# One pool of twelve 1024-column tiles for raw, upper and lower weights, in a two-layer hybrid decoder trunk

## The chip, the cores and the metric

The kernel runs on one core of a Trainium2 chip. The core has five engines with an instruction queue each, which this document calls by the profile's names: PE (matmuls; PEld is its weight load, which overlaps), DVE (vector), ACT (scalar), POOL (GpSimd) and SP, whose queue issues nearly all transfers between device memory (HBM) and the on-chip memory (SBUF). Each engine works through its queue in order; semaphores hold an instruction back until what it reads is there or what it overwrites is free. PE's sums go to a third memory (PSUM).

The metric is the device time of one execution in microseconds. The kernel before was run three times: 1729.38, 1731.37 and 1731.99 us, so the median is 1731.37 us.

## The reference

The input is 512 tokens of 1024 float32 numbers; 16 learned tokens are put ahead, so layer 0 and the beginning of layer 1 work on 528 tokens.

```python
for i in range(DEPTH):                       # two layers
    mix = retention_gdn_mixer(h, ...) if i % 2 == 0 else mamba2_mixer(h, ...)
    h = layer_norm(DN_ALPHA * h + mix, ln1_w[i], ln1_b[i])
    h = layer_norm(DN_ALPHA * h + sq_relu_mlp(h, mlp_w1[i], mlp_w2[i]), ln2_w[i], ln2_b[i])
return h[:, N_META:]
```

`retention_gdn_mixer` projects the tokens to 6 x 1024 + 8 columns, runs four retention heads and four gated delta-rule heads in chunks, and projects 2048 columns back to 1024. `mamba2_mixer` projects to 5152 columns, puts 3072 of them through a convolution of four taps and a silu, runs a chunked decay attention in four groups of eight heads (state 128), gates, normalises and projects 2048 columns back. `sq_relu_mlp` is `square(relu(h @ w1)) @ w2` with 4096 hidden columns. All weights are float32 and are read once: some 150 MB.

## The kernel before

**How a product is made.** Everything is kept feature-major: a tile has 128 features as partitions and the tokens as columns. A float32 operand is split into an upper part `hi`, which is the number cast to PE's shorter float32r format, and a lower part `lo`, which is the number minus `hi`, again as float32r. A product of 128 x 128 weights with the tokens is then three matmuls into one PSUM tile (`mm3`): upper weight by upper input (line 173), upper weight by lower input (line 174), lower weight by upper input (line 175). The program has 3296 such triples for its large products, each for 272, 256 or 512 tokens.

**How a weight comes in.** The host lays the weights out so that one load brings 128 x 1024 numbers (512 KB): eight blocks of 128 x 128, which are the eight k-steps of one output tile. `fetch` (line 155) takes a raw tile `wr` (tag of two buffers of 1024 columns) and issues the load on SP. `wload` (line 160) takes the raw tile in two halves of 512 columns; for each it takes an upper tile `wh` and a lower tile `wl` (six buffers of 512 columns each) and calls `split`: a cast on ACT (line 152) and a subtraction on DVE (line 153). There are 253 loads: 245 of 1024 columns, six of 512 columns (lines 1158 and 1164), one of 256 and one of 64. The same `split` is used, outside `wload`, for the input tokens (line 253) and the gated heads (line 920).

**What sets the order.** The kernel is written as one program in which large products (`phase`, `product`) are cut into units; between two units `tick` lets every pending generator emit its next stage (heads, norms, state updates), so that PE has matmuls while other engines prepare a stage. The program is then planned when it is built: a planner plays it through with assumed durations, puts each engine's instructions in the order in which they become ready (earlier ones in the program first), hands out the buffers of a tag in the program's order of first use, and writes the semaphore waits. The durations of the tiles' instructions and the number of buffers thus decide not only waits but the order of every queue.

**Buffers of the weights.** A raw buffer is free again when its two subtractions are done. A `wh` buffer is free when its last upper-weight matmul (line 174) is done, a `wl` buffer when its last lower-weight matmul (line 175) is done. With two raw buffers and six half tiles of each kind, at most two loads are under way or waiting and at most three weight tiles are split. Together these buffers take 8 + 12 + 12 = 32 KB of each SBUF partition. (Lines 70 to 82 give the other tags: 40 tiles `s`, 20 `m`, 40 `n`, 3 `row`; PSUM has three tiles `pmm` and five `pmx`.)

**The stages, in the order of time.** Loads of tokens and first weights, with some matmuls of zeros (to 8 us); layer 0's projections with the heads beside them (to about 400 us); output projection and norm (to 545 us); MLP 0 (to 890 us); norm and layer 1's projections (`conv_tile`, `z_tiles`) with the four groups of the decay attention (`ssd_group`, line 967) beside them (to about 1255 us); output projection, norm, MLP 1 (to 1700 us), and the last norm with the stores.

**The group stage, which the prediction needs.** A conv tile's product goes from PSUM through ACT (`conv_evac`, line 400), ACT (line 405), three multiply-adds on DVE (line 407), ACT (line 408) and DVE (line 410); its result feeds PE transposes, from which DVE makes `xdt` (line 1006). The decays of a chunk come by a load (`row<-rd`), POOL (line 985), ACT (lines 986 and 987) and POOL (line 1001). Then PE makes the chunk's products (lines 1045 and 1049). There are four groups of four chunks, 16 chunks in all. The weight casts and subtractions of the conv tiles stand in the same ACT and DVE queues.

Of the kernel before, what the change touches and what calls it, by code (L numbers as in the profile page):

```python
# [18 lines left out]
P = 128  # L19
# [38 lines left out]
def trunk(ctx: ExitStack, tc: tile.TileContext, a, out):  # L58
# [34 lines left out]
    # ---------------------------------------------------------------- interleaving  # L93
    # The large products are cut into units; between two units every pending task (a generator) emits
    # its next stage, so that the tensor engine works on while other engines prepare a stage's inputs.
# [31 lines left out]
    # ---------------------------------------------------------------- constants  # L127
# [22 lines left out]
    # ---------------------------------------------------------------- weights  # L150
# [3 lines left out]

    def fetch(src, n=1024):
        raw = sb.tile([P, 1024], F32, tag="wr", bufs=2, name=nm("wr"))
        SY.dma_start(raw[:, :n], src)
        return raw

    def wload(src, n=1024, raw=None):  # L160
        if raw is None:
            raw = fetch(src, n)
        res = []
        for i in range(0, n, 512):
            c = min(512, n - i)
            hi = sb.tile([P, 512], F32R, tag="wh", bufs=6, name=nm("wh"))
            lo = sb.tile([P, 512], F32R, tag="wl", bufs=6, name=nm("wl"))
            split(hi[:, :c], lo[:, :c], raw[:, i:i + c])
            res.append((hi, lo))
        return res  # L170
# [6 lines left out]
    def product(o, blks, xs, m=P, k0=0, k1=None, every=8):  # L177
        """o[m, n] += sum over k0 <= k < k1 of blks[k]^T xs[k]"""
        per = 512 // P if m == P else 8
        n = len(xs)  # L180
        for k in range(k0, k1 or n):
            hi, lo = blks[k // per]
            c = (k % per) * m
            mm3(o, (hi[:, c:c + m], lo[:, c:c + m]), xs[k], k == 0, k == n - 1)
            if k % every == every - 1 and k < n - 1:
                tick()

    def phase(tiles, rhs, evac, ns, head=0, tail=0, ready=None):
        """tiles: list of (srcs, key[, m]); rhs[half][k] = (hi, lo) APs, rhs[2] both halves where they fit a
        bank. In the first and the last tiles the halves are apart, so that what precedes and follows can  # L190
        work on one half at a time."""
# [28 lines left out]
    def jobs(lst, rhs, ns, **kw):  # L220
        """phase whose tiles bring their own evac"""
        phase(lst, rhs, lambda ev, hf, o: ev(hf, o), ns, **kw)

    # ---------------------------------------------------------------- h: hi/lo in two halves
# [3 lines left out]
    def parts(pair, spans):  # L228
        """(hi, lo) over the spans of both tiles"""
        return [tuple(x[:, o:o + n] for x in pair) for o, n in spans]  # L230

    # while the first loads are under way, products of zeros let the clock of the tensor engine come up
# [26 lines left out]
    def layernorm(r, ns, hf, go, apply, together=False):  # L259
        """statistics of the tokens of a half as its sums r come, then apply(off, bn, pt, mean, rstd, i)"""  # L260
# [49 lines left out]
    def norm_after(r, ns, wcol, bcol):  # L310
        """tasks for both halves, each from when its sums have been emitted"""
# [35 lines left out]
    def residual(hx, offs, ns, early=()):  # L347
        """evac into r = alpha * h + product"""
# [48 lines left out]
    # ---------------------------------------------------------------- shared pieces  # L397
# [15 lines left out]
    def conv_job(src, wc, bcol, done):  # L413
        """projection through conv and silu, feature-major [128, L]"""
        cin = tl("s", L + 3)
        G.memset(cin[:, 0:3], 0.0)

        def evac(hf, o):
            conv_evac(cin, hf, o)
            if hf == 1:  # L420
                done(conv_silu(cin, wc, bcol))

        return [src], evac
# [21 lines left out]
    def gate_job(src, width, task):  # L445
        """small projection, then a task on its sums"""
# [10 lines left out]
    def gate_task(fm, width):  # L457
        """token-major [128, 5, width] with unused rows zero"""
# [9 lines left out]
    def decay(dt_in, bias, alog, nh):  # L468
        """g = -exp(A_log) softplus(x + bias), sums over chunks and their exponentials"""
# [17 lines left out]
    # ================================================================ layer 0 mixer  # L487
# [15 lines left out]
    # scratch in DRAM for the diagonal blocks of 32: a pitch of 129 rows makes the 68 blocks equidistant  # L503
# [26 lines left out]
    def gdn_keys(hd):  # L530
# [3 lines left out]
        # decays between the tokens of a chunk  # L534
# [16 lines left out]
        # similarities of the keys; the squared norms are on their diagonal  # L551
# [32 lines left out]
    def gdn_base():  # L584
        """diagonal blocks of 32, one to a partition: forward substitution"""
# [349 lines left out]
    # ================================================================ layer 1 mixer  # L935
# [27 lines left out]
    def hb(ap):  # L963
        """[128, heads] over the 64 features of a head"""
        return bc(ap, 64)
# [188 lines left out]
    # the first products begin with the groups that are ready  # L1154
# [20 lines left out]
    def finish(hf):  # L1175
# [16 lines left out]
        def last(blocks):  # L1192
            """both blocks at once, over the engines; what needs the mean alone comes first"""
# [27 lines left out]
# ---------------------------------------------------------------- host side: layout only  # L1221
def _tiles(w, cols):
    """[K, M] -> [M tiles, 128, K] in tiles of 128 columns"""
# [95 lines left out]
```

## Time and profile before

| | us |
|---|---|
| three runs | 1729.38, 1731.37, 1731.99 |
| span of the profiled execution, first to last instruction | 1727.4 |
| PE busy | 1690.1 |
| DVE busy | 1015.5 |
| ACT busy | 680.0 |
| POOL busy | 324.1 |

The span of the profiled execution is 4.0 us below the median of the runs; start and end of an execution, outside the span, are in the runs' times and not in the span. In the page, "busy" is the time in which an engine has an instruction under way. A group is a line of the source on one engine with the tiles that it writes and reads, how often, its busy time, the mean of one, and the idle time of the engine just before it with what ended that idle time. The trace also tells, for any stretch of time, how long each engine was busy in it, and which clock PE was granted (1.00 is full speed).

### The profile page before, as it was taken

How to read it: one execution, taken by the hardware profiler on the slowest of the kernel's cores; microseconds unless marked ns; L12 is line 12 of the kernel's file. 1: busy time of each engine (PE TensorE's matmuls, PEld its weight loads, DVE VectorE, ACT ScalarE, POOL GpSimd, SP SyncE). 2: the span in 40 equal slices, each digit the busy share in tenths (PEclk: the TensorE clock that was granted, in tenths of full speed). 3: DMA queues.
4: the chain of work that ended last, by engine and by line, in shares of the span. 5: the costliest groups of instructions: out<-in, count | busy, mean ns of one | idle time of the engine just before them, and what ended most of it. 6: DMA issues, size and time to landing. Idle time of an engine off the chain costs nothing.

```text
span 1727.4 us, 29456 instructions
## 1 busy us (share of the span) xinstructions
PE 1690.1 (98%) x11644; PEld 1537.0 (89%) x11644; DVE 1015.5 (59%) x2116; ACT 680.0 (39%) x1455; POOL 324.1 (19%) x380
## 2 busy tenths in 40 slices
PE   9999999999999999999999999999999999999997
PEld 8899998899999999999999878888788888888886
DVE  6896667676436443343348767868753744444345
ACT  4432345554225333242425634554432533333331
POOL 1311211010004111010202245242400411101012
PEclk9999999999999999999999999999999999999999
DMA  7224211112222222222221443333222222222221
GB/s 252 69 86 121 77 63 62 38 63 85 98 66 82 92 92 87 98 87 89 96 72 61 131 133 88 99 110 111 80 79 98 73 86 98 98 98 89 94 98 61
DMA packets 80325, 157.99 MB, mean 91 GB/s; under 512 B 12668, under 2 KB 45820, under 8 KB 79932
## 3 DMA queue, kind: packets, MB, share of 16 engines
q1 hardware_dynamic: 80044, 155.86, 28.2%
q8 instruction: 91, 1.49, 0.4%
q14 instruction: 46, 0.38, 0.1%
q10 hardware_dynamic: 144, 0.26, 0.0%
HBM read 149.95 MB, written 6.15 MB: 90 GB/s over the span
## 4 chain that ended last, share of the span: by engine, by line
PE 84%; DVE 6%; DMA 3%; POOL 3%; ACT 2%; issue 2%; SPq 0%; POOLq 0%; DVEq 0%; ACTq 0%
PE pmm L173 24%; PE pmm L175 24%; PE pmm L174 24%; DMA row<-rd 2%; DVE s L407 2%; DVE wl L153 2%; POOL row L985 1%; PE pmx L271 1%; POOL hl L341 1%; DMA wr<-in_w 1%; PE pmx L331 1%; PE pmx L1049 1%; PE pmx L1045 1%; POOL n L147 1%; PE pmx L753 1%
## 5 line engine op out<-in xcount | busy, mean ns | idle before, releaser
L173 PE MATMUL pmm<-hh,wh 128*128 128x272 f32 (+4 forms) x2104 | 652.3, 311 | 2.3 <-ACT wh L152 0.9
L174 PE MATMUL pmm<-hl,wh 128*128 128x272 f32 (+4 forms) x2104 | 638.5, 304 | 2.7 <-POOL hl L341 2.1
L175 PE MATMUL pmm<-hh,wl 128*128 128x272 f32 (+4 forms) x2104 | 640.3, 304 | 0.1
L153 DVE TENSOR_TENSOR wl<-wr,wh 128x512 fp32r<-128x512 f32 (+1 forms) x498 | 376.2, 759 | 319.8 <-ACT wh L152 313.5
L152 ACT CAST wh<-wr 128x512 fp32r<-128x512 f32 (+1 forms) x498 | 306.6, 619 | 628.3 <-PE pmm L174 605.1
L173 PEld LDWEIGHTS pmm<-hh,wh 128*128 128x128 f32 (+2 forms) x2104 | 393.5, 187 | 25.0 <-issue 4.4
L174 PEld LDWEIGHTS pmm<-hl,wh 128*128 128x128 f32 (+2 forms) x2104 | 393.6, 187 | 24.4 <-POOL hl L341 4.6
L175 PEld LDWEIGHTS pmm<-hh,wl 128*128 128x128 f32 (+2 forms) x2104 | 393.5, 187 | 17.0 <-DVE wl L153 0.3
L173 PE MATMUL pmm<-s,wh 128*128 128x256 f32 (+2 forms) x1192 | 377.9, 317 | 0.0
L175 PE MATMUL pmm<-s,wl 128*128 128x256 f32 (+2 forms) x1192 | 377.2, 317 | 0.0
L174 PE MATMUL pmm<-s,wh 128*128 128x256 f32 (+2 forms) x1192 | 376.4, 316 | 0.0
L174 PEld LDWEIGHTS pmm<-s,wh 128*128 128x128 f32 x1192 | 224.3, 188 | 15.5 <-DVE s L1124 0.3
L173 PEld LDWEIGHTS pmm<-s,wh 128*128 128x128 f32 x1192 | 224.4, 188 | 15.1
L175 PEld LDWEIGHTS pmm<-s,wl 128*128 128x128 f32 x1192 | 224.1, 188 | 15.0
L383 POOL TENSOR_TENSOR m<-m 128x256 f32<-128x256 f32 (+1 forms) x128 | 92.1, 729 | 536.0 <-ACT m L381 532.7
L147 POOL TENSOR_TENSOR n<-n,neg 128x1 f32<-128x1 f32 (+2 forms) x58 | 37.9, 657 | 462.7 <-DVE n L146 436.5
L390 DVE TENSOR_TENSOR s<-m,s 128x256 fp32r<-128x256 f32 (+1 forms) x128 | 64.3, 521 | 95.2 <-POOL m L383 93.2
L407 DVE SCALAR_TENSOR_TENSOR s<-s,pp,s 128x528 f32<-128x528 f32 x120 | 96.5, 804 | 25.8 <-ACT s L405 24.1
L363 DVE TENSOR_TENSOR m<-m,pmm 128x256 f32<-128x256 f32 (+1 forms) x108 | 43.7, 423 | 107.4 <-PE pmm L175 107.2
L381 ACT ACTIVATE m<-pmm 128x256 f32<-128x256 f32 (+1 forms) x128 | 48.7, 380 | 60.4 <-PE pmm L175 60.4
L985 POOL TENSOR_TENSOR row<-row,m 128x1024 f32<-128x1024 f32 x16 | 32.8, 2052 | 122.3 <-DMA row<-rd 78.3
L389 ACT ACTIVATE s<-m 128x256 fp32r<-128x256 f32 (+1 forms) x128 | 54.0, 422 | 3.9
(275 smaller groups left out, 1501.1 us busy)
## 6 DMA issues: line engine op xcount, KB each, us to landing
wr<-in_mw SPq DMA_DIRECT2D x128, 512.0 KB, 3.3
wr<-in_w SPq DMA_DIRECT2D x88, 512.0 KB, 3.3
wr<-in_wo SPq DMA_DIRECT2D x29, 512.0 KB, 3.5
row<-rd SPq DMA_DIRECT2D x16, 512.0 KB, 6.0
s<-rd SPq DMA_DIRECT2D x32, 128.0 KB, 6.1
out<-row SPq DMA_DIRECT2D x7, 256.0 KB, 2.0
wr<-in_wo SPq DMA_DIRECT2D x6, 256.0 KB, 3.0
dt<-row SPq DMA_DIRECT2D x3, 365.5 KB, 5.9
```

The lines of the kernel that those rows point to most:

```text
L147: G.tensor_tensor(dst, t, neg5[0:part, 0:n], op=POW)
L152: S.copy(dst_hi, src)
L153: V.tensor_tensor(dst_lo, src, dst_hi.bitcast(F32), op=SUB)
L173: T.matmul(o, w[0], x[0], start=first, stop=False)
L174: T.matmul(o, w[0], x[1], start=False, stop=False)
L175: T.matmul(o, w[1], x[0], start=False, stop=last)
L381: S.activation(t, o, AF.Relu)
L383: G.tensor_tensor(q, t, t, op=MUL)
L389: S.activation(hi, t, AF.Square)
L390: V.tensor_tensor(lo, q, hi.bitcast(F32), op=SUB)
L407: V.scalar_tensor_tensor(acc, cin[:, k:k + L], w[k], acc, op0=MUL, op1=ADD)
L985: G.tensor_tensor(g3(rw, 8), g3(rw, 8), bc(gc[:, c * 32 + 8 * g:c * 32 + 8 * g + 8], P), op=SUB)
```

## The change

The raw, upper and lower tiles of the weights get one common tag, `w`, of twelve buffers of 1024 columns. `wload` casts a whole weight tile by one ACT instruction and subtracts it by one DVE instruction, and hands out views of 512 columns, so `product` is not changed. `fetch` takes its raw tile from the same tag. The twelve buffers take 48 KB of each partition in place of 32 KB; the 16 KB come from a smaller reserve for dynamic transfers (`dynamic_dma_scratch_size=1024` in the last hunk). The rest of the diff takes comments out, which moves line numbers and nothing else.

```diff
+    def wtile(dt=F32R):
+        return sb.tile([P, 1024], dt, tag="w", bufs=12, name=nm("w"))
+
     def fetch(src, n=1024):
-        raw = sb.tile([P, 1024], F32, tag="wr", bufs=2, name=nm("wr"))
+        raw = wtile(F32)
         SY.dma_start(raw[:, :n], src)
         return raw
 
+    def halve(raw, n=1024):
+        hi, lo = wtile(), wtile()
+        split(hi[:, :n], lo[:, :n], raw[:, :n])
+        return [(hi[:, i:i + 512], lo[:, i:i + 512]) for i in range(0, n, 512)]
+
     def wload(src, n=1024, raw=None):
-        if raw is None:
-            raw = fetch(src, n)
-        res = []
-        for i in range(0, n, 512):
-            c = min(512, n - i)
-            hi = sb.tile([P, 512], F32R, tag="wh", bufs=6, name=nm("wh"))
-            lo = sb.tile([P, 512], F32R, tag="wl", bufs=6, name=nm("wl"))
-            split(hi[:, :c], lo[:, :c], raw[:, i:i + c])
-            res.append((hi, lo))
-        return res
+        return halve(fetch(src, n) if raw is None else raw, n)
...
-    nc = bacc.Bacc("TRN2", target_bir_lowering=False, num_devices=1)
+    nc = bacc.Bacc("TRN2", target_bir_lowering=False, num_devices=1, dynamic_dma_scratch_size=1024)
```

## The prediction

> **What bounds the kernel now.** I read the page first, then the groups by form, then the waits, then busy time by stretches, and last the timeline where PE stood still.
>
> ```profile
> PE 1690.1 (98%) x11644; PEld 1537.0 (89%) x11644; DVE 1015.5 (59%) x2116; ACT 680.0 (39%) x1455; POOL 324.1 (19%) x380
> L153 DVE TENSOR_TENSOR wl<-wr,wh 128x512 fp32r<-128x512 f32 x496 | 375.6, 760 | 318.0 <-ACT wh L152 311.6 <-PE pmx L1120 2.1 <-PE pmx L638 0.7
> L152 ACT CAST wh<-wr 128x512 fp32r<-128x512 f32 x496 | 305.9, 620 | 617.2 <-PE pmm L174 594.4 <-DMA wr<-in_w 11.3 <-DMA wr<-in_wo 3.6
> L173 PE MATMUL pmm<-hh,wh 128*128 128x272 f32 x832 | 243.6, 293 | 0.9 <-ACT wh L152 0.9
> L175 PEld LDWEIGHTS pmm<-hh,wl 128*128 128x128 f32 x2072 | 390.3, 188 | 16.5 <-DVE wl L153 0.3
> SPq L157 <- DVE wl L153: 1253.8, 207, 21.4
> ```
>
> PE is busy for 98% of the span. The change deletes no matmul, so at most the 1727.4 - 1690.1 = 37.3 us in which PE is not busy can be won, plus what a lowered clock costs. The rows of the weights look alarming and are not: ACT stands 594.4 us before its casts, but what it waits for is line 174 on PE, the last reader of the buffer that the cast will overwrite; and SP stands 1253.8 us for line 153, which frees the raw buffer. These are producers held back by full buffers. In the other direction PE's matmuls wait 0.9 us for a cast, and its weight loads 0.3 us for a subtraction. More buffers for a producer that is ahead already win nothing by themselves.
>
> The stretches show where the 37.3 us lie.
>
> ```profile
> 0.00:20.00 20.00, 16.82 (x110) 12.51 (x111) 8.68 (x24) 10.56 (x26) 1.28 (x9) 1.00 0.83 262
> 545.00:890.00 345.00, 345.00 (x2832) 344.82 (x2831) 142.22 (x261) 119.53 (x240) 44.52 (x63) 1.00 0.28 91
> 970.00:1255.00 285.00, 269.24 (x1831) 231.83 (x1832) 220.37 (x351) 139.35 (x271) 116.02 (x91) 0.98 0.35 101
> 1370.00:1700.00 330.00, 330.00 (x1458) 268.75 (x1457) 143.85 (x261) 115.03 (x239) 42.30 (x60) 1.00 0.28 94
> 1700.00:1727.40 27.40, 16.41 (x134) 15.32 (x132) 16.17 (x38) 3.55 (x5) 10.14 (x10) 0.88 0.20 77
> ```
>
> After the time come PE, PEld, DVE, ACT and POOL busy, PE's clock, the share of the transfer engines and GB/s. In the two MLPs (rows two and four) PE never stops. It loses 3.2 us at the start, 11.0 us at the end, where no weight is left to load, and 285.00 - 269.24 = 15.8 us in the group stage, at a mean clock of 0.98. So the change is decided in the start and in the group stage.
>
> **The change part by part.** *Fewer, longer instructions.* The 245 full tiles lose one cast and one subtraction each. Their lengths:
>
> ```profile
> L152 ACT CAST s<-m 128x256 fp32r<-128x256 f32 x16 | 6.5, 408 | 14.6 <-DVE m L914 14.6
> L153 DVE TENSOR_TENSOR s<-m,s 128x256 fp32r<-128x256 f32 x16 | 6.8, 423 | 3.2 <-ACT s L152 3.1
> L986 ACT ACTIVATE row<-row 128x1024 f32<-128x1024 f32 x16 | 17.0, 1063 | 46.4 <-POOL row L985 44.8 <-POOL s L416 1.6
> 545.00:890.00 345.00, 82.73 (x120) 1.00 0.28 91
> 970.00:1255.00 285.00, 76.67 (x69) 0.98 0.35 101
> ```
>
> The last two rows are line 153 alone: 82.73 / 120 = 0.69 us in MLP 0, but 76.67 / 69 = 1.11 us in the group stage. From 256 to 512 columns a cast grows by 0.62 - 0.41 = 0.21 us, so 1024 columns take 0.62 + 2 x 0.21 = 1.04 us (the row of line 986, the same width on ACT, has 1.06). A subtraction grows by 0.69 - 0.42 = 0.27, so 0.69 + 2 x 0.27 = 1.23 us. Per tile ACT saves 2 x 0.62 - 1.04 = 0.20 us and DVE 2 x 0.69 - 1.23 = 0.15 us, over 245 tiles 49 and 37 us. In the MLPs that is worth nothing: PE is full there, and these engines have over half of their time free. Should PE ever wait there, an evacuation behind a cast would come up to 1.04 - 0.62 = 0.42 us later.
>
> *The group stage.* Why a subtraction takes 1.11 us there, and what it delays, the timeline shows (DVE and POOL, start, duration).
>
> ```profile
> 1060.44 2.84 POOL L1001 TENSOR_TENSOR row<-row,m 128x1024 f32<-128x1024 f32 x1 [1.68 <-DVE m L996]
> ...
> 1060.96 2.87 DVE L153 TENSOR_TENSOR wl<-wr,wh 128x512 fp32r<-128x512 f32 x1
> ...
> 1064.44 0.68 DVE L153 TENSOR_TENSOR wl<-wr,wh 128x512 fp32r<-128x512 f32 x1
> 1065.22 0.71 DVE L410 SCALAR_TENSOR_TENSOR s<-s,s 128x528 f32<-128x528 f32 x1
> 1065.85 0.68 DVE L1006 TENSOR_TENSOR s<-pmx,m 128x512 f32<-128x512 f32 x1
> ...
> 1066.67 0.48 PE L1045 MATMUL pmx<-row,s 128*64 128x128 f32 x2 [3.87 <-DVE s L1006]
> ```
>
> The first half beside POOL's line 1001 ended 0.55 us after it and took 2.87 us, not 0.69: DVE stood until POOL was done. Two halves of weights, which nobody needed yet, stood ahead of lines 410 and 1006, and PE stood 3.87 us for line 1006. There are six such places (five for line 1006, one for line 410); in the six us ahead of each, line 153 took:
>
> ```profile
> 966.00:972.00 6.00, 1.96 (x2) 1.00 0.90 239
> 1004.00:1010.00 6.00, 0.90 (x2) 1.00 0.25 87
> 1060.60:1066.60 6.00, 3.70 (x3) 0.91 0.09 11
> 1098.00:1104.00 6.00, 1.59 (x1) 1.00 0.27 87
> 1160.60:1166.60 6.00, 0.77 (x2) 1.00 0.28 87
> 1178.70:1184.70 6.00, 1.53 (x1) 1.00 0.28 87
> sum 36.00, DVE 10.44; mean DVE 1.74
> ```
>
> That is 10.44 us. A collision costs 1.11 - 0.69 = 0.42 us per instruction, and half as many instructions begin: 34.5 x (1.23 + 0.42) = 56.9 us in place of 76.67, a factor of 0.74. On these paths it takes off 0.26 x 10.44 = 2.7 us. The bounds are -10.44 (no subtraction in front any more, since the new order puts each tile elsewhere) and +0.54 (1.23 - 0.69) at each place where a whole tile now stands and half a tile stood before. I take 2.7, the value between.
>
> *The start* pays for whole tiles. Rows of ACT, DVE, PE and its weight load:
>
> ```profile
> 7.66 0.62 ACT L152 CAST wh<-wr 128x512 fp32r<-128x512 f32 x1 [1.22 <-DMA wr<-in_w]
> 8.31 0.69 DVE L153 TENSOR_TENSOR wl<-wr,wh 128x512 fp32r<-128x512 f32 x1 [1.40 <-ACT wh L152]
> 8.33 0.40 PE L173 MATMUL pmm<-hh,wh 128*128 128x272 f32 x1 [0.95 <-ACT wh L152]
> 9.05 0.19 PEld L175 LDWEIGHTS pmm<-hh,wl 128*128 128x128 f32 x1 [0.32 <-DVE wl L153]
> 18.43 1.14 ACT L152 CAST wh<-wr 128x512 fp32r<-128x512 f32 x2 [1.77 <-DMA wr<-in_w]
> 19.40 0.39 PE L173 MATMUL pmm<-hh,wh 128*128 128x272 f32 x1
> ```
>
> The first weight lands, is cast and is used at once. Line 173 starts 1.04 - 0.62 = 0.42 us later; line 175 waits for 7.66 + 1.04 + 1.23 = 9.93 in place of 9.05, so up to 0.9 us later, with matmuls of the eight-column gate product as cover (up to 0.5 us). The second weight, landed at 18.43, is used at 19.40: its cast would end at 19.47 and its subtraction at 20.7 where line 175 now starts at 19.83; 0 to 0.9 us. Between 0.4 and 1.8 I take 1.0 us, since both places have a little cover.
>
> *The common pool.* First uses come in the order raw, upper, lower, raw, and so on, so twelve buffers are four tiles in three forms, or five split tiles and a raw one when raws are freed early, where there were three split tiles and two raws. PE's 0.9 + 0.3 us of waits are at the start, where no buffer is short, so depth wins nothing. What moves is who frees a raw buffer: a full pool gives the next load a buffer that PE has finished, not one that DVE has subtracted. Loads in flight take a median of 3.3 us in a tile time of 24 matmuls by 256 and 24 by 272, 5.9 us (345.00 us hold 60 tiles, 5.75 each). I cost it at nothing, under the cover of the four tiles ahead; without it, see the third rival. The smaller reserve costs nothing either: it serves no queue that the page shows moving the kernel's data, which is hardware_dynamic.
>
> *Sum.* 1727.4 + 1.0 - 2.7 = 1725.7 for the span; the median of the runs lies 4.0 above the span, so **1729.7 us**, or 1.7 us below the median.
>
> **The rivals.** *Cover only.* The planner's order keeps the critical lines where they are late, and only the start pays: 1731.4 + 1.0 = 1732.4 us. For it speaks that POOL and loads also end waits in that stage (line 1045 waited 6.3 us for POOL); against it that 10.44 us of line 153 stand in plain sight.
>
> *All of it.* The new order frees all six places. The clock comes back too. These rows show a stop of 2.04 us, PE's clock after it, and the clock after the stop of 3.87 us:
>
> ```profile
> 1010.02 0.44 PE L1045 MATMUL pmx<-row,s 128*64 128x128 f32 x4 [2.04 <-DVE s L1006]
> ...
> 1010.00:1020.00 10.00, 9.98 (x54) 0.83 0.63 163
> 1067.00:1080.00 13.00, 13.00 (x91) 0.79 0.46 129
> ```
>
> That is 0.17 x 10 + 0.21 x 13 = 4.4 us more: 1731.4 + 1.0 - 10.4 - 4.4 = 1717.6 us. (The Trainium skill, TensorE: Matmul & The Clock Gate, Part 1, has the clock halve after an idle window of about 3.4 us. The second row agrees; the first follows a stop of 2.04 us, which that rule would let pass, and by the rule alone this case would be 1.7 us worse, 1719.3.)
>
> *Blocks in the way: slower.* DVE can't put line 410 or 1006 between two halves any more. In each of the 16 chunks a whole tile may stand ahead of line 1006 where half a tile does: 16 x 0.54 = 8.6 us, with the start 1731.4 + 1.0 + 8.6 = 1741 us. Since 2.7 - 1.0 = 1.7 us are won, this turns the sign from four chunks on, and passes 0.2% from ten on. For it speaks that the order is planned with durations that know no collision (2.87 us above); against it that line 1006 waits at five of 16 chunks only. The Trainium skill speaks for this case (Perfetto Trace Analysis, Optimizing Scalar/DVE Operations): grouping pays where the engine is saturated, and where it isn't but makes bubbles elsewhere, instructions should be broken up. With DVE at 59% over the span the rule says slower; at 220.37 of 285.00, 77%, in the stage that counts, the row lies between its two halves.
>
> *Casts that wait for loads: slower.* If the pool is full, the load starts when PE leaves a tile, and a cast that is planned too early holds ACT, with lines 400, 405 and 408 of the conv chain behind it. Weight loads take 3.3 us at the median, and those of `row<-rd` on the same queue 6.0; 2.7 us at two chunks is 5.4: 1731.4 + 1.0 + 5.4 = 1738 us. Against it: ACT waits 11.3 + 3.6 us for loads now.
>
> ```profile
> wr<-in_w SPq DMA_DIRECT2D x88, 512.0 KB, 3.3
> row<-rd SPq DMA_DIRECT2D x16, 512.0 KB, 6.0
> ```
>
> **How the numbers follow.** Forecast 0.42 (own range 1725.5 to 1732.5), cover only 0.14, all of it 0.18, blocks in the way 0.16, casts behind loads 0.10. This kernel's runs can tell about 0.2% from no change, 3.5 us: faster is below 1727.9, slower above 1734.8. Faster takes the whole third case and 0.14 of the forecast, 0.32; same takes 0.28 of the forecast and the 0.14 of cover only, 0.42; slower the last two, 0.26. The range goes from 1717 to 1740: it leaves out some 0.08 below and some 0.10 above.
>
> **What would show it.** Right: lines 152 and 153 with 245 instructions each on 1024 columns at 1.04 and 1.23 us in the MLPs, both MLPs with PE never idle, the start 0.4 to 1.8 us longer, line 153 in the group stage near 57 us, and PE's idle time there below 15.8 us by some 3 us. Wrong: PE idle behind line 153 or 152 outside the start; ACT waiting tens of us for loads of `w`; line 1045 waiting longer for line 1006 than 9.3 us; or a change in a stage that this text holds to be covered.

## The result, and the profile after

| | before | after |
|---|---|---|
| runs, us | 1729.38, 1731.37, 1731.99, 1729.34 | 1738.32, 1741.04, 1740.47, 1736.55 |
| median, us | 1730.38 | 1739.39 |
| ratio | | 1.0053, 95% interval 1.0038 to 1.0068 |

The kernel became slower by 9.0 us. The profiled execution of after took 1738.32 us, with a span of 1736.2 us. Behind line 153 the lines of after have numbers one lower than before: 172 to 174 are the three weight matmuls, 830 is the copy that was line 831, 1005 was 1006.

First the page of after: busy time and instructions of each engine, and the group of the casts (busy time, mean ns of one, and the idle time before them).

```profile
PE 1693.3 (98%) x11644; PEld 1540.9 (89%) x11644; DVE 963.9 (56%) x1871; ACT 642.0 (37%) x1210; POOL 338.0 (19%) x380
L152 ACT CAST w<-w 128x1024 fp32r<-128x1024 f32 (+2 forms) x253 | 261.0, 1032 | 469.0 <-DMA w<-in_mw 289.9
```

Measured by busy time the change did what it says: 245 instructions fewer on each of two engines, DVE down by 51.6 us, ACT by 38.0. The idle time has changed its reason. Casts waited for PE to free a buffer before; now they wait for their load. The waits of after (total, times, longest) by the tensor that is loaded:

```profile
ACT w L152 <- DMA w<-in_mw: 289.9, 85, 7.5
ACT w L152 <- DMA w<-in_wo: 70.4, 19, 8.9
ACT w L152 <- DMA w<-in_w: 42.4, 20, 14.3
```

The largest of these is harmless and the smallest is not. `in_mw` is loaded for the MLPs, `in_wo` for the output projections, `in_w` for the two mixers. The stretches of after (columns as in the prediction):

```profile
140.00:165.00 25.00, 17.53 (x118) 16.32 (x117) 11.03 (x27) 3.43 (x7) 3.82 (x5) 0.80 0.45 103
554.00:900.00 346.00, 346.00 (x2838) 345.83 (x2839) 131.76 (x203) 107.36 (x184) 51.74 (x65) 1.00 0.27 91
980.00:1265.00 285.00, 269.77 (x1848) 232.91 (x1847) 198.20 (x320) 139.02 (x240) 125.10 (x91) 0.99 0.37 103
1380.00:1710.00 330.00, 330.00 (x1459) 268.88 (x1458) 132.02 (x199) 104.11 (x176) 45.55 (x59) 1.00 0.27 91
```

The MLPs (second and fourth row) are at 346.00 of 346.00 and 330.00 of 330.00 us. From 140 to 165 us PE is busy for 17.53 of 25 us, and the clock falls to 0.80. Before, the same stretch was full:

```profile
140.00:165.00 25.00, 24.94 (x187) 23.06 (x186) 16.98 (x42) 6.67 (x16) 3.30 (x6) 1.00 0.49 136
```

The timeline of after shows what happens there (start, duration, engine, what ended the idle time; SPq is SP's queue of transfers).

```profile
138.29 5.00 SPq L605 DMA_DIRECT2D du<-row  x1
145.29 5.43 SPq L612 DMA_DIRECT2D row<-dt  x3
150.59 0.38 PE L822 MATMUL pmx<-cst,s 128*128 128x128 f32 x2
154.04 0.84 SPq L160 DMA_DIRECT2D w<-in_w  x2
158.29 1.04 ACT L152 CAST w<-w 128x1024 fp32r<-128x1024 f32 x1 [14.34 <-DMA w<-in_w]
159.37 1.23 DVE L153 TENSOR_TENSOR w<-w,w 128x1024 fp32r<-128x1024 f32 x1 [8.58 <-ACT w L152]
159.40 0.38 ACT L830 COPY m<-pmx 128x256 f32<-128x256 f32 x1
159.83 2.08 PE L809 MATMUL pmx<-s,s 128*128 128x128 f32 x8 [7.47 <-ACT m L830]
```

Read from below: PE stands 7.47 us at line 809, which waits for the copy of line 830 on ACT. By the source, line 809 reads nothing that the copy writes. What it needs is one of the five PSUM tiles `pmx`, and the copy frees one by reading it. The copy takes 0.38 us, and its input, made by line 822, was there from 151 us on. But at the head of ACT's queue stands the cast of the 23rd weight tile, and that cast waits 14.34 us for a load. The load is issued at 154.04 only, because SP's queue has the forward substitution's transfers in front: two writes, then reads that wait for them. So a cast that nobody needed yet held a copy that everybody needed. The same tile held a second queue: its subtraction on DVE waited 8.58 us for the cast, and line 854, the state's multiply-add, which reads another `pmx` tile, stood behind it until 160.51.

Before, the same transfers were as slow, and nobody minded:

```profile
131.90 5.33 SPq L606 DMA_DIRECT2D du<-row  x1
137.33 6.48 SPq L157 DMA_DIRECT2D wr<-in_w  x1
146.10 0.37 ACT L831 COPY m<-pmx 128x256 f32<-128x256 f32 x1 [3.98 <-PE pmx L823]
148.71 0.36 ACT L831 COPY m<-pmx 16x256 f32<-16x256 f32 x1 [2.07 <-DVE m L829]
149.45 0.62 ACT L152 CAST wh<-wr 128x512 fp32r<-128x512 f32 x1 [0.39 <-PE pmm L174]
```

The load at 137.33 is that of the 22nd tile, and the cast at 149.45 its first half. Here the cast waits for PE (line 174), the last reader of one of the six `wh` buffers. The planner reckons with that wait and puts the cast behind the copies. Counted in ACT's queue, the 23rd tile's cast stands behind seven copies of line 831 before, and behind four of line 830 after: with buffers for more tiles it was planned three copies earlier.

Where the 9 us arise is seen when the runs are laid side by side. For each profiled execution the table has the time at which PE had begun as many columns of weight products as before's profile had begun at the mark, minus the mark (us; positive is late). The last column compares the spans. It holds most of the experiments too.

| at, us | 82 | 140 | 158 | 514 | 944 | 1110 | 1272 | end |
|---|---|---|---|---|---|---|---|---|
| after | 4.9 | 4.9 | 14.5 | 14.8 | 12.4 | 13.5 | 10.1 | 8.9 |
| scratch | 3.5 | 3.5 | 3.5 | 3.5 | 3.5 | 4.0 | 3.7 | 3.7 |
| m_own | 6.8 | 7.6 | 7.6 | 8.2 | 11.8 | 16.2 | 11.8 | 11.5 |
| p_half | 1.8 | 1.8 | 12.5 | 13.5 | 11.3 | 9.2 | 5.3 | 4.1 |
| raw_own | 7.7 | 10.1 | 10.1 | 10.9 | 9.0 | 11.9 | 10.7 | 10.9 |
| after_anchor | 5.1 | 5.1 | 5.0 | 5.8 | 3.1 | 3.8 | 0.3 | -1.0 |
| after_anchor_start | 1.1 | 1.1 | 1.0 | 2.0 | -0.6 | 0.2 | -2.7 | -4.0 |
| p_half_anchor | 1.2 | 1.2 | 1.1 | 2.5 | 0.2 | -1.9 | -5.9 | -7.1 |
| mlp_whole | 1.2 | 1.2 | 1.1 | 2.5 | -0.4 | -2.6 | -6.6 | -7.9 |
| group_whole | 2.2 | 2.2 | 2.1 | 3.5 | 1.5 | 6.8 | 3.6 | 2.8 |
| group_pool | 0.0 | 0.0 | -0.1 | 1.2 | -0.8 | 0.2 | -3.1 | -3.9 |

After loses 4.9 us up to 82 us and 9.6 us between 140 and 158 us; between 514 and 944 it gets 2.4 back, in the norm ahead of MLP 0, in the group stage (944 to 1272) another 2.3, and 1.2 behind it. With 0.3 us between 158 and 514 that is 4.9 + 9.6 + 0.3 - 2.4 - 2.3 - 1.2 = 8.9 us. The row of `scratch` is a warning. That kernel has before's instructions in the same order on every engine, and its profile is 3.5 us late at 82 us: the start alone differs by as much from one execution to another. What is said of the start below rests on medians.

### The profile page after: what moved, and what is told of

Read it like the earlier page. It is cut to its first block, busy times and chain, and to the rows that moved or that the text cites. A ratio compares the mean times of both kernels' runs of the same rounds, so it can differ in the third digit from the quotient of the medians.

```text
span 1736.2 us, 28669 instructions
## 1 busy us (share of the span) xinstructions
PE 1693.3 (98%) x11644; PEld 1540.9 (89%) x11644; DVE 963.9 (56%) x1871; ACT 642.0 (37%) x1210; POOL 338.0 (19%) x380
## 4 chain that ended last, share of the span: by engine, by line
PE 86%; DVE 4%; DMA 4%; POOL 3%; ACT 2%; issue 1%; SPq 0%; POOLq 0%; DVEq 0%; ACTq 0%
PE pmm L172 25%; PE pmm L174 25%; PE pmm L173 25%; DMA row<-rd 2%; DVE s L406 1%; PE pmx L270 1%; PE pmx L1044 1%; POOL row L984 1%; DMA du<-row 1%; DVE w L153 1%; DMA w<-in_w 1%; PE pmx L1048 1%; POOL n L147 1%; POOL hl L340 1%; PE pmx L752 1%
## 5 line engine op out<-in xcount | busy, mean ns | idle before, releaser
L172 PE MATMUL pmm<-hh,w 128*128 128x272 f32 (+4 forms) x2104 | 655.1, 312 | 1.8 <-ACT w L152 1.2
L174 PE MATMUL pmm<-hh,w 128*128 128x272 f32 (+4 forms) x2104 | 642.3, 306 | 0.4 <-DVE w L153 0.4
L173 PE MATMUL pmm<-hl,w 128*128 128x272 f32 (+4 forms) x2104 | 640.5, 305 | 1.0 <-DVE hl L153 0.4
L153 DVE TENSOR_TENSOR w<-w,w 128x1024 fp32r<-128x1024 f32 (+2 forms) x253 | 318.3, 1259 | 354.5 <-PE pmm L173 292.5
L152 ACT CAST w<-w 128x1024 fp32r<-128x1024 f32 (+2 forms) x253 | 261.0, 1032 | 469.0 <-DMA w<-in_mw 289.9
L172 PEld LDWEIGHTS pmm<-hh,w 128*128 128x128 f32 (+2 forms) x2104 | 395.4, 188 | 24.1 <-issue 4.2
L173 PEld LDWEIGHTS pmm<-hl,w 128*128 128x128 f32 (+2 forms) x2104 | 395.5, 188 | 22.5 <-issue 2.3
L174 PEld LDWEIGHTS pmm<-hh,w 128*128 128x128 f32 (+2 forms) x2104 | 395.4, 188 | 18.1 <-DVE w L153 1.1
L172 PE MATMUL pmm<-s,w 128*128 128x256 f32 (+2 forms) x1192 | 378.3, 318 | 0.0
L174 PE MATMUL pmm<-s,w 128*128 128x256 f32 (+2 forms) x1192 | 377.4, 317 | 0.0
L173 PE MATMUL pmm<-s,w 128*128 128x256 f32 (+2 forms) x1192 | 376.4, 316 | 0.0
L173 PEld LDWEIGHTS pmm<-s,w 128*128 128x128 f32 x1192 | 224.4, 188 | 15.4 <-DVE s L1123 0.3
L172 PEld LDWEIGHTS pmm<-s,w 128*128 128x128 f32 x1192 | 224.5, 188 | 14.7
L174 PEld LDWEIGHTS pmm<-s,w 128*128 128x128 f32 x1192 | 224.2, 188 | 14.9
L382 POOL TENSOR_TENSOR m<-m 128x256 f32<-128x256 f32 (+1 forms) x128 | 102.1, 806 | 529.0 <-ACT m L380 523.1
```

The source lines that it names most:

```text
L152: S.copy(dst_hi, src)
L153: V.tensor_tensor(dst_lo, src, dst_hi.bitcast(F32), op=SUB)
L172: T.matmul(o, w[0], x[0], start=first, stop=False)
L173: T.matmul(o, w[0], x[1], start=False, stop=False)
L174: T.matmul(o, w[1], x[0], start=False, stop=last)
L382: G.tensor_tensor(q, t, t, op=MUL)
```

## The experiments

### The two halves of the change, apart

Two theories stood against each other. Q: the common pool changes the order of the queues, and the order makes the stop. B: the longer blocks of 1.04 and 1.23 us delay DVE-heavy layer 0. `m_own` is before with the merged split alone, in buffers of the same total size:

```diff
+        hi = sb.tile([P, 1024], F32R, tag="wh", bufs=3, name=nm("wh"))
+        lo = sb.tile([P, 1024], F32R, tag="wl", bufs=3, name=nm("wl"))
+        split(hi[:, :n], lo[:, :n], raw[:, :n])
```

> Only the merged cast and subtraction, with tags of their own (raw 2, hi 3, lo 3, of 1024 columns, the same 32 KB as before). In the kernel after, TensorE stops 7.6 us at 152-160 us: the cast of the 23rd weight tile stands in ScalarE's queue for 14.3 us, ahead of two copies that TensorE needs, and its load was issued only at 154 us, behind SP's reads for the merges. Theory Q (the common pool brings that order of the queues): the stop is absent here, and the gains in the group stage and the norms stay: 1719 to 1728 us. Theory B (longer blocks of 1.04 and 1.23 us delay layer 0): the loss is here too, 1735 to 1741 us.

1740.6 us, ratio 1.0048 (1.0035 to 1.0061). `p_half` is after with the split in halves, so the pool alone:

```diff
-        split(hi[:, :n], lo[:, :n], raw[:, :n])
+        for i in range(0, n, 512):
+            s = slice(i, min(i + 512, n))
+            split(hi[:, s], lo[:, s], raw[:, s])
```

> Only the common pool of 12, the split in halves of 512 as before. Theory Q: the stop of several us before the similarity of the second retention head is here, with the cast waiting for its load: 1733 to 1743 us. Theory B: about the time before, 1728 to 1732 us.

1733.0 us, ratio 1.0012 (1.0004 to 1.0021). Its timeline:

```profile
155.43 1.14 ACT L152 CAST w<-w 128x512 fp32r<-128x512 f32 x2 [14.57 <-DMA w<-in_w]
156.07 0.69 DVE L153 TENSOR_TENSOR w<-w,w 128x512 fp32r<-128x512 f32 x1 [8.89 <-ACT w L152]
156.68 0.41 DVE L856 SCALAR_TENSOR_TENSOR m<-m,pmx 128x256 f32<-128x256 f32 x1
157.15 0.58 PE L811 MATMUL pmx<-s,s 128*128 128x128 f32 x1 [8.83 <-DVE m L856]
```

Each theory was half right. The stop belongs to the pool: it is there with halves (14.57 us before the cast, 8.83 us of PE) and, as the table shows, not in `m_own`. What ends PE's stop here is DVE's line 856 (854 in after), which stands right behind the subtraction of the late tile. The pool alone ends only 2.1 us above before, for it also won: in `p_half` the norm ahead of MLP 0 gained 2.2 us and the group stage 6.0 (11.3 to 5.3) without any merging. The merged split alone costs as much as the whole change, and elsewhere: 7.6 us up to 140 us and 3.6 us between 514 and 944.

`raw_own` gives raw tiles a tag of two and leaves ten buffers to the others:

```diff
-        return sb.tile([P, 1024], dt, tag="w", bufs=12, name=nm("w"))
+        return sb.tile([P, 1024], dt, tag="w", bufs=10, name=nm("w"))
...
-        raw = wtile(F32)
+        raw = sb.tile([P, 1024], F32, tag="wr", bufs=2, name=nm("wr"))
```

> After, but with raw tiles in a tag of their own (2) and a pool of 10 for hi and lo; 12 buffers in all. SP still has the reads of the merges ahead of the next weight load, and ScalarE that load's cast ahead of the copies. Theory Q: the stop stays, 1733 to 1742 us. If it is the sharing of the pool between raw and the split tiles itself and not the order of the queues, the stop goes: 1722 to 1730 us. Theory B: 1735 to 1741 us.

1738.3 us, ratio 1.0041 (1.0028 to 1.0054): a time that Q expected as well as B, but not for Q's reason. There is no stop of several us at 150 to 160 (the table moves by 0.0 from 140 to 158). In SP's queue the 23rd load stands ahead of the writes here (140.67 us, the first write 141.25), and its cast, with four copies ahead of it as in after, waited 2.42 us for a buffer and not for its load. This kernel loses in the start and by small stops.

`scratch` is before with `dynamic_dma_scratch_size=1024` and nothing else.

> Before, with only the smaller reserve for DMA descriptors. Theories Q and B: no change, 1728 to 1733 us. If the reserve matters: 1735 us or more.

1730.7 us, ratio 1.0001 (0.9993 to 1.0010). The smaller reserve costs nothing.

### Three attempts to bring the load forward

If the late load makes the stop, an earlier load should end it. In `p_half_p4` and `after_p4` the reads are started two ticks later, which puts the 23rd load ahead of them in SP's queue; `before_p4` has the same edit on before.

```diff
-        yield from pause(2)
+        yield from pause(4)
         tms = [tl("row", 1024) for _ in range(2)]
```

> The common pool with the split in halves, and the task that reads the merges' blocks back is started two ticks later, which puts the 23rd weight load ahead of these reads in SP's queue. Theory Q (the stop of 9.0 us at 157 us comes from that order alone): the stop goes, and the pool's gains of some 2 us at the norm before the first MLP, 6 us in the group stage and 1 us at the second norm stay: 1720 to 1726 us, faster than before. If the wait moves elsewhere: 1730 to 1734 us.

> The kernel after, with the same later start of the reads. Theory Q: the stop of 7.6 us at 160 us goes, 1728 to 1733 us; what is left against the pool with halves (3 to 8 us) is then the price of the longer cast and subtraction in the start and the group stage. If the stop is due to the longer blocks, it stays: 1736 to 1741 us.

> The kernel before with the same two ticks; there the load in question is ahead of the reads already. Theory Q: no change, 1729 to 1733 us. If the two ticks help by themselves, 1724 to 1728 us.

1731.0 us (ratio 1.000, 0.999 to 1.001), 1739.1 us (1.0050, 1.0035 to 1.0065) and 1733.1 us (1.0012, 1.0002 to 1.0022). Beside before nothing was won, and the stop stayed: 7.89 us of PE in `p_half_p4`, 7.19 in `after_p4`. The timeline of `after_p4`:

```profile
144.26 6.29 SPq L160 DMA_DIRECT2D w<-in_w  x1
153.81 1.04 ACT L152 CAST w<-w 128x1024 fp32r<-128x1024 f32 x1 [8.72 <-DMA w<-in_w]
154.88 1.23 DVE L153 TENSOR_TENSOR w<-w,w 128x1024 fp32r<-128x1024 f32 x1 [9.23 <-ACT w L152]
159.29 0.40 DVE L854 SCALAR_TENSOR_TENSOR m<-m,pmx 128x256 f32<-128x256 f32 x1
159.74 0.58 PE L809 MATMUL pmx<-s,s 128*128 128x128 f32 x1 [7.19 <-DVE m L854]
```

The load was issued ahead of the reads, at 144.26 us, and landed late all the same, for the two writes were still under way in the same queue. This refuted Q as it was put: not the reads alone, but whatever of the forward substitution lies ahead. It shows a second thing. The cast ran 4.5 us earlier than in after, and the copy behind it was through at 155 us, yet PE stood until 159.74. What it waited for was DVE: the subtraction had held DVE's queue for 9.23 us, and behind it seven more instructions (lines 778 to 863) had to be made up for before line 854 could free its `pmx` tile. So the late tile holds two queues, ACT's by its cast and DVE's by its subtraction. The rates of after (from 138 to 158 us, half a us each) show the writes as the long run of 44 GB/s:

```profile
GB/s 36 38 48 53 53 49 44 44 44 43 44 43 43 44 44 44 44 44 44 43 44 44 44 44 95 183 293 329 320 314 95 5 92 288 226 232 319 279 336 385
```

Side by side with these ran `mlp_whole_p4`, with the merged split in the MLPs alone, on top of `p_half_p4` (the flag `whole` is set in `mlp` and cleared behind it):

```diff
+        step = n if whole else 512
+        for i in range(0, n, step):
+            s = slice(i, min(i + step, n))
```

> As the pool with halves and the later reads, but in the two MLPs (128 of the 245 full tiles) a tile is split by one cast and one subtraction. Prediction's claim that the removed fixed costs are worth nothing there: within 1 us of the pool with halves and the later reads. If the long blocks cost anything in the MLPs: 1 to 5 us more; if the removed 0.1 us of DVE per tile were worth something: up to 13 us less.

1730.8 us beside 1731.0: in the MLPs merging is worth nothing in either sign.

Next the writes were made shorter. `after_dense` and `before_dense` write the same bytes as rows of 4 KB. The reads that follow still fetch blocks, so these two kernels do not compute the decoder; they serve for their times alone.

```diff
+    def dense(d):
+        v = d[:, :, :]
+        return bass.AP(v.tensor, v.offset, [[32 * P + 32, 68], [1, 1024]])
...
-        SY.dma_start(diag(dt_), tb)
+        SY.dma_start(dense(dt_), tb)
```

and the same for `du`.

> After, but the two results of the forward substitution go to DRAM as rows of 4 KB instead of as 32x32 blocks in packets of 128 B (the blocks read back are then not the right ones, so the output of layer 0's first half is not the reference's). In the profile of after the two writes hold the DMA queue from 138 to 154 us at 44 GB/s, and the weight load whose cast heads ScalarE's queue lies behind them. Theory W (the writes hold the load, its early cast holds ScalarE, and the copies behind it hold TensorE): the stop of 7.6 us at 160 us goes, 1728 to 1733 us. Theory B (the longer blocks in layer 0): the stop stays, 1736 us or more.

> Before with the same change of the writes (the same part of the output is not the reference's). Theory W: the load behind the writes is not missed there, since its cast stands later in ScalarE's queue: no change, 1728 to 1733 us.

1737.2 us (ratio 1.0032, 1.0020 to 1.0044) and 1731.4 us (0.9999, 0.9990 to 1.0007). The timeline of `after_dense`:

```profile
153.53 1.04 ACT L152 CAST w<-w 128x1024 fp32r<-128x1024 f32 x1 [9.79 <-DMA w<-in_w]
154.90 0.58 PE L813 MATMUL pmx<-s,s 128*128 128x128 f32 x1 [3.69 <-ACT m L834]
```

Half of the expected effect on the stop: PE's fell from 7.47 to 3.69 us, the cast's wait from 14.34 to 9.79. The time fell by 2.2 us beside after and so stayed where theory B had put it, above 1736. The writes now ran at some 90 GB/s. (The Trainium skill, DMA: Bandwidth & Descriptors, Specifications, asks for transfers of at least 512 B to reach line rate; the 128 B packets at 44 GB/s beside 90 GB/s for 4 KB rows agree in direction.) Before did not care, as expected.

`after_actq` and `p_half_actq` let ACT issue the two writes, so that SP's loads needn't lie behind them:

```diff
-        SY.dma_start(diag(dt_), tb)
+        S.dma_start(diag(dt_), tb)
```

> The common pool with the split in halves; the two writes are issued by ScalarE, so that weight loads on SP's queue need not lie behind them. Theory W: the stop of 9 us at 157 us goes or shrinks under 2 us; 1721 to 1726 us, faster than before. If ScalarE's issue of the writes (5 us for the second one on SP) takes the place of the wait: 1728 to 1734 us.

> After with the two writes issued by ScalarE. Theory W: 1729 to 1733 us; what then stands between this and the pool with halves and the same writes (3 to 8 us) is the price of the merged cast and subtraction in the start and the group stage. Theory B: 1736 us or more.

1733.9 us (ratio 1.0013, 1.0005 to 1.0022) and 1738.6 us (1.0040, 1.0028 to 1.0053). Both times lie where the expectations had put a failure. The 23rd load now came earlier (its cast ran at 144.96 us), and the next tile took over its part. The timeline of `after_actq`:

```profile
160.21 1.04 ACT L152 CAST w<-w 128x1024 fp32r<-128x1024 f32 x1 [13.86 <-DMA w<-in_w]
161.58 0.24 PE L813 MATMUL pmx<-s,s 128*16 128x16 f32 x2 [7.62 <-ACT m L830]
```

The load of the 24th tile lay behind the reads, its cast was again at the head of ACT's queue, and PE stood 7.62 us. Whichever load came too late, the cast stood there to wait for it.

### The place of one cast

So the place of the cast was left. `after_anchor` holds the casts of the 23rd and 24th tile in ACT's queue behind the copies behind which before has them (`halved` is the old body of `halve`). Buffers, transfers and lengths stay as in after.

```diff
+    copies, tiles = [], []
+
     def halve(raw, n=1024):
+        tiles.append(raw)
+        k = {22: 6, 23: 7}.get(len(tiles) - 1)
+        if k is not None:
+            with tc.issue_after(copies[k]):
+                return halved(raw, n)
+        return halved(raw, n)
...
-            S.copy(vt[:n], pv[:n, 0:256])
+            copies.append(S.copy(vt[:n], pv[:n, 0:256]).ins)
```

> After, but the casts of the 23rd and 24th weight tile are held in ScalarE's queue behind the seventh and eighth of the retention's copies, which is where the kernel before has them (after has them behind four and five); transfers and buffers stay. Theory P (the place of the cast): no stop over 1.5 us between 140 and 170 us, 1729 to 1733 us. If a TensorE wait for the late weight tile takes its place: a stop of 3 to 8 us there, 1735 to 1740 us.

1728.6 us, ratio 0.9989 (0.9979 to 0.9999). Its timeline and its stretch:

```profile
151.18 0.37 ACT L840 COPY m<-pmx 128x256 f32<-128x256 f32 x1 [7.05 <-PE pmx L832]
153.68 0.36 ACT L840 COPY m<-pmx 16x256 f32<-16x256 f32 x1 [1.97 <-DVE m L838]
155.35 9.42 SPq L160 DMA_DIRECT2D w<-in_w  x3
162.33 1.05 ACT L152 CAST w<-w 128x1024 fp32r<-128x1024 f32 x1
163.41 1.23 DVE L153 TENSOR_TENSOR w<-w,w 128x1024 fp32r<-128x1024 f32 x1 [0.82 <-ACT w L152]
```

```profile
140.00:165.00 25.00, 25.00 (x187) 22.97 (x186) 16.05 (x43) 3.97 (x11) 5.07 (x7) 1.00 0.45 104
```

The load is issued even later than in after (155.35), the cast runs four us later (162.33), and PE is busy for 25.00 of 25 us: the copies went through at 151 and 153 us. The median fell by 10.8 us (1739.4 to 1728.6). This settles that the stop came from the place of these two tiles' splits in the queues. The hold names ACT's queue alone, but the subtraction comes after its cast, so in DVE's queue it moved too: it runs at 163.41, behind the line that is 854 in after (150.96 here). Which of the two queues counts for how much was not tried apart.

`p_half_anchor` is `p_half` with the same hold.

> The common pool with the split in halves and the same place of the two casts. Theory P: no stop there, and the pool's gains at the norms and in the group stage stay: 1720 to 1726 us, faster than before by 0.3 to 0.6%. Otherwise 1730 to 1734 us.

1721.7 us, ratio 0.9946 (0.9931 to 0.9960). **This version beats both kernels**, before by 0.5% and after by 1.0%: the common pool is a gain of some 9 us once the order it brings is mended, and merging takes from it.

### What the merged split costs

Run side by side, `after_anchor` was 6.9 us slower than `p_half_anchor`; they differ by the merged split alone. `after_anchor_start` has halves for the first twelve tiles:

```diff
-        split(hi[:, :n], lo[:, :n], raw[:, :n])
+        step = n if len(tiles) > 12 else 512
+        for i in range(0, n, step):
+            s = slice(i, min(i + step, n))
+            split(hi[:, s], lo[:, s], raw[:, s])
```

> As after_anchor, but the first twelve tiles (0 to 82 us) are split in halves as before. By the rows of the runs so far the merged split costs some 4 us up to 82 us (the pool kernels with one cast are at 4.7 to 6.0 us there against the time before, those with halves at 0.1 to 1.8): 3 to 5 us less than after_anchor, 1725 to 1729 us. If the start's difference is the chance of when loads land: within 1 us of after_anchor.

1725.4 us, ratio 0.9968 (0.9956 to 0.9981): by the medians 3.2 us of the 6.9 arise in the start. The runs of the two overlap (1723.1 to 1728.4 and 1727.4 to 1733.1), so the size is known to some 3 us only. `mlp_whole` and `group_whole` are `p_half_anchor` with the merged split in the MLPs alone, and between the two MLPs alone (the flag as above).

> As p_half_anchor, but with the merged split in the two MLPs alone. Prediction's step for the MLPs (worth nothing, in both signs): within 1 us of p_half_anchor, 1720.5 to 1722.8 us. If a longer block costs there too: over 1723 us.

> As p_half_anchor (pool, halves, the two casts held back), but from the end of the first MLP to the start of the second the split is one cast and one subtraction. Prediction's step for the group stage (the shorter subtraction brings L1006 forward and is worth 2.7 us there): 1718 to 1720 us. The opposite, as read from the profiles so far (the merged split gives back 3 to 4 us of what the pool gains there): 1724 to 1727 us.

1722.3 us (ratio 0.9955, 0.9943 to 0.9968) and 1726.2 us (0.9977, 0.9967 to 0.9986), run side by side. The MLPs cost nothing that is clear of noise; layer 1's mixer costs 3.9 us more. (The Trainium skill, Perfetto Trace Analysis, Optimizing Scalar/DVE Operations, lets grouping pay where the engine is saturated; with DVE at 56% in after nothing was gained by it, which agrees.) Why it costs, a view of GpSimd and DVE in `group_whole` suggests (this execution took 1732.3 us, 6.1 above the kernel's median, so its stops may be longer than usual):

```profile
1078.56 1.90 POOL L1000 TENSOR_TENSOR row<-row,m 128x1024 f32<-128x1024 f32 x1 [5.22 <-PE pmm L189]
1080.45 1.04 POOL L1073 TENSOR_TENSOR s<-s,s 128x512 f32<-128x512 f32 x1
1081.53 0.69 DVE L1074 TENSOR_TENSOR s<-s,pmx 128x512 f32<-128x512 f32 x1 [3.85 <-POOL s L1073]
1091.03 0.87 PE L1060 MATMUL pmx<-row,s 128*64 128x128 f32 x5 [2.85 <-DVE s L1021]
```

and in `p_half_anchor`, where line 1073 is 1069 and line 1000 is 996:

```profile
1069.69 1.28 POOL L1069 TENSOR_TENSOR s<-s,s 128x512 f32<-128x512 f32 x1
1073.98 1.90 POOL L996 TENSOR_TENSOR row<-row,m 128x1024 f32<-128x1024 f32 x1 [3.00 <-DMA row<-rd]
```

The state's product, which DVE waits for, is first there; in `group_whole` it stands behind a decay product that waits 5.22 us. `group_pool` swaps the two by hand:

```diff
+            decayed.append(c)
+            with ExitStack() as st:
+                if len(decayed) - 1 == 8:
+                    st.enter_context(tc.issue_after(states[4]))
                 G.tensor_tensor(g3(rw, 8), g3(rw, 8), bc(gc[:, c * 32 + 8 * g:c * 32 + 8 * g + 8], P), op=SUB)
...
+                states.append(G.tensor_tensor(g3(Sn, 8), g3(St, 8), hb(setot[:, c, hs]), op=MUL).ins)
```

> As group_whole (merged split in layer 1's mixer), but at the one place at 1078 us the state's product is held ahead of the decay product in GpSimd's queue, as it stands with the split in halves. If the cost of the merged split there is this order: 2 to 4 us less than group_whole, 1722 to 1724 us, and the stop of 3.0 us at 1091 us goes. If it is the longer blocks: within 1 us of group_whole, 1725 to 1727 us, the stop stays.

1724.4 us, ratio 0.9961 (0.9947 to 0.9975). The timeline of `group_pool` at the corresponding place:

```profile
1087.29 0.55 PE L1064 MATMUL pmx<-row,s 128*64 128x128 f32 x6 [1.22 <-DVE s L1025]
```

PE's stop fell from 2.85 to 1.22 us, and the median by 1.9 us, to between what was expected of the order and what of the longer blocks. The intervals of the two ratios overlap, and the stops are of one execution each. So that the order is a part of the 3.9 us is not shown, and the rest was not traced.

## Why the prediction was wrong

Forecast were 1729.7 us and no clear change; measured is 1739.4, slower by 0.53%.

**The bound: right.** PE stays the bound at 98%, and no weight matmul's mean time changed by more than 2 ns.

**Lengths of the merged instructions: right.** The step said 1.04 and 1.23 us. The casts of after read 1.04 and 1.05; line 153 alone in after's stretches gives 73.51 / 60 = 1.23 us in MLP 0:

```profile
554.00:900.00 346.00, 73.51 (x60) 1.00 0.27 91
980.00:1265.00 285.00, 53.97 (x35) 0.99 0.37 103
```

That this is worth nothing in the MLPs holds as well (`mlp_whole`). Over the span, busy time fell by 38.0 us on ACT and 51.6 on DVE, where 49 and 37 had been worked out.

**The group stage: right sum, wrong cause.** The step said that line 153 falls to 56.9 us there (53.97 measured) and that this wins 2.7 us (2.3 by the table); that the sum came out is luck. For the pool alone wins 6.0 with halves (`p_half`; 6.1 in `p_half_anchor`), the merged split alone nothing (`m_own` goes from 11.8 to 11.8), and on top of the pool it costs 3.9 (`group_whole` beside `mlp_whole`). The factor of 0.74 is a fact of busy time. It hardly shortened PE's wait for line 1006 (by 0.8 us, where the pool with halves took off 3.7), as the waits of before, after and `p_half` show (total, times, longest):

```profile
PE pmx L1045 <- DVE s L1006: 9.3, 6, 3.9
PE pmx L1044 <- DVE s L1005: 8.5, 4, 4.6
PE pmx L1046 <- DVE s L1007: 5.6, 3, 4.5
```

Merged blocks alone leave 8.9 us (`m_own`). Nor did the sign come that the prediction named: PE's idle time in the stretch from 980 to 1265 us is 285.00 - 269.77 = 15.2 us, not some 3 under 15.8. What came forward came by the pool: in `p_half_anchor` line 153 has

```profile
965.00:1250.00 285.00, 62.09 (x66) 0.98 0.37 104
```

which is 0.94 us each beside 1.11 before, with halves as before. That fewer of them met POOL, or met it shorter, is a guess; why the pool's order does that was not tried.

**The start: the term of 1.0 us was mis-sized.** It measured 3.2 us by medians (`after_anchor` against `after_anchor_start`, the first twelve tiles). The working took the later cast and subtraction at two places and left out the clock and what follows. The stretch from 8 to 12 us has in after

```profile
8.00:12.00 4.00, 3.16 (x12) 2.06 (x13) 3.39 (x8) 3.08 (x9) 0.00 (x0) 0.50 0.99 289
```

and in before

```profile
8.00:12.00 4.00, 3.59 (x26) 1.00 0.99 283
```

Half the clock for four us. In `scratch`, with before's own order, the same four us ran at

```profile
8.00:12.00 4.00, 2.72 (x16) 0.87 0.97 290
```

so a part of this is chance, and the profile that the prediction was worked out from had caught a good start (its execution took 1729.38 us, 2.0 less than the median that the forecast was set to). From 38 to 82 us after falls back by another 2.2 us (by the account of the table), `after_anchor_start` by 0.4. The timeline of after has a stop there behind DVE:

```profile
57.92 0.20 PE L545 MATMUL pmx<-cst,n 16*16 16x16 f32 x2 [2.98 <-DVE n L537]
```

Line 537 comes at 57.55 us in after and at 51.75 in `after_anchor_start` (line 550 there). In DVE's queue the same work stands ahead of it in both but for the weights: eight whole tiles in after, 14 halves there.

**The common pool at nothing, "under the cover of the four tiles ahead": this is the step that failed.** It cost 9.6 us between 140 and 158 us, and 10.8 us came back when the two tiles were held. The reasoning was that depth neither wins nor hurts. It did both: the 6.0 us of the group stage are the pool's too. And it moved the casts of the weights forward in ACT's queue, three copies ahead of where PE's pace had kept them, with their subtractions in DVE's. These queues are worked through in order, so they passed the late load on to what stood behind. The prediction had this very mechanism as a rival with a chance of 0.10 and 1738 us; it put it into the group stage, priced it by the landing time of single loads, and took ACT's small waits for loads (11.3 + 3.6 us) as evidence against it. These waits were small because the full buffers before held the casts back: the change took that brake away. What was missing in the search was the place where SP's queue carries something long, the forward substitution's two writes, which the page's totals do not show. That the rival's time lies near the measured one is luck: two stops of 2.7 us in the group stage were meant, and one of 7.5 us in layer 0 came.

**Blocks in the way, at 1741 us: not the cause of the stop.** The stop is there with halves, and goes with merged blocks once the cast is held. But merged blocks do cost: 9.7 us without the pool (`m_own`), and with it 3.9 us in layer 1's mixer, the place that the rival named, where it had 8.6. Whether they cost by standing ahead of line 1006 was not tried.

**The tests named.** "ACT waiting tens of us for loads of `w`" came true, but 289.9 of the 402.7 us are harmless. The sharper test would have been the longest such wait, 14.3 us, and what stands behind that cast.

## What to carry to other kernels

A buffer limit is also a brake: here it kept the casts of weights that were not needed yet from the head of an in-order queue. Before giving a producer more buffers, look for what stands behind it on its engine, and behind its consumer on the next one, and for the longest transfer that its load can be caught behind. And where a planner orders the queues, judge a change by its order at the few late places: here holding two tiles' casts back won 10.8 us where 89.6 us of saved busy time won nothing, and with the split left in halves it gave a version 0.5% faster than the kernel before.

## What the runs showed of the hardware

In the four us from 8 to 12 the granted clock was 0.50 in after, with PE busy for 3.16 of them and a longest stop of 1.17 us (line 172 at 8.63 us). It was 1.00 in before, with a stop of 0.95 us, and 0.87 in the same order run again (`scratch`), with one of 1.48 us.

The Trainium skill (TensorE: Matmul & The Clock Gate, Part 1) has the clock halve after about 3.4 us without work; no single stop up to 12 us is as long in these three executions. So in a start with several short stops the halved clock must be reckoned with, and a start should be judged by several executions: the same order differed by 3.5 us between two of them.

Two writes of 272 KB each in packets of 128 B kept one queue at some 44 GB/s for about 12 us, and a weight load issued behind them landed 9.5 us after its issue (`after_p4`: issued at 144.26, cast at 153.81), where the median is 3.3 us.
